# Down projection of 18 of 22 feature tiles as 2x2 blocks in 7 products, in one pipeline with the up projection

## The chip, the core and the metric

The kernel runs on one core of a Trainium2 chip. The metric is the device time of one execution, in microseconds (us). The kernel before takes 2363.89 us, the median of 3 runs that lie between 2362.02 and 2364.42 us.

## What is computed

Two layers on 1024 tokens of width 1024, in fp32. Each layer has a mixer (gated MLP and pooling in layer 0, two kinds of attention in layer 1) and a feed-forward part, with residual sums and norms between them. The change is in the feed-forward part alone:

```python
def conv_ffn(h, w_up, conv_w, conv_b, w_down):
    a, g = jnp.split(h @ w_up, 2, axis=-1)              # w_up: 1024 x 5632
    a = lax.conv_general_dilated(a, conv_w, ...) + conv_b   # causal, 3 taps per feature
    return (jax.nn.gelu(a) * g) @ w_down                # w_down: 2816 x 1024
...
h = h + conv_ffn(rms_norm(h, norm_ffn[layer]), ...)
```

The 2816 features are 22 tiles of 128.

## The kernel before

Activations lie with features on the partitions and tokens along the free axis. An fp32 product is made of three matmuls (`mm3`, L164 to L168): each operand x is split into hi, a rounded copy, and lo = x - hi, and hi·hi, hi·lo and lo·hi are summed in PSUM. The hi part is a ScalarE cast and the lo part a VectorE subtraction (`split`, L177 and L178, for activations; L355 and L359 for the weights of the up projection; L136 and L137 for other weights). A matmul has 128x128 weights and 512 tokens.

**Up** (`up`, L468). One step per feature tile j computes gate and value of that tile together, as a 2x2 block product in 7 instead of 8 products (`PRODUCTS`, L404). The blocks of the activations (b11, b21, d, e, t3, b22, t4) are sums of quarters of the normed input, made once per layer; the four combinations of weights ("forms" 0 to 3, `form`, L361) are made in each step for the next one. A product is 4 contraction tiles x 3 = 12 matmuls, a step 84. The order of products is 1, 2, 4, 3, 6, 5, 7, and `read` (L421) moves results out of PSUM between them. Behind product 7 comes `conv` (L450: two ScalarE passes, two VectorE passes), and in the next step, behind product 2, `gate` (L459), which multiplies by the gate and writes the 512 KB tile to `a_dram` in DRAM (L465). Steps 0 and 1 run interleaved while the blocks are made, parts of steps 2 and 3 (`early`) with them; from j = 2 on a loop runs the steps one after the other.

**Down.** The 22 tiles are taken in chunks of 2, 4, 4, 4, 4, 4. `fetch(c)` (L556) reads a chunk's tiles from `a_dram` and splits them, `down(c)` (L565) runs the plain product: 8 output tiles x 2 halves of the tokens x the chunk's tiles x 3 matmuls, and after each output tile's half a VectorE add of the PSUM bank into the residual tile x (L582). `residual` (L549) loads x, 16 transfers of 256 KB, in the last up step. In that step the first two fetches and the first weights are issued too. The last chunk also feeds the next norm.

All transfers named here are issued by SyncE (SP) in program order, and each waits there until its target buffer is free. A tile framework places each engine's instructions in an order that it works out from the program and its own cost estimates; ScalarE, VectorE, TensorE and SP each run theirs strictly in that order.

Layer 0's feed-forward lies at about 242 to 924 us of the trace, layer 1's at about 1660 to 2360 us. The last up step of layer 0 runs from 666.0 to 685.06 us, that of layer 1 from 2082.6 to 2101.7 us.

Of the kernel before, what the change touches and what calls it, by code (L numbers as in the profile page):

```python
# [10 lines left out]
F32 = mybir.dt.float32  # L11
F32R = mybir.dt.float32r
# [10 lines left out]
HF = 512  # L23
FF = 2816
NFF = FF // P
CHUNKS = (2, 4, 4, 4, 4, 4)
EPS = 1e-6
NEG = -1.0e30
LAMBDA_INIT = 0.8 - 0.6 * math.exp(-0.3)
# [31 lines left out]
def tile_block(  # L61
# [58 lines left out]
    a_dram = dram.tile([NFF, P, S], F32, name="a_dram")  # L120


    def w_tiles():
# [2 lines left out]
    class Weights:  # L126


        def __init__(self, src, ncol=2048):
            self.w = ncol // 2  # L130
            self.parts = []
            for i in range(2):
                raw = wraw_p.tile([P, self.w], F32, tag="raw", name="raw")
                nc.sync.dma_start(raw, src[:, i * self.w : (i + 1) * self.w])
# [132 lines left out]
    class FFN:  # L267
        def __init__(self, layer, stack):
            self.layer = layer
            hp = stack.enter_context(pool(name=f"ffh{layer}", bufs=1))  # L270
            self.raw_p = stack.enter_context(pool(name=f"ffr{layer}", bufs=4))
# [72 lines left out]
        def raw(self, j):  # L344
            f = self.forms[j] = {}
            for i, x in enumerate("ag"):
                f[x] = self.raw_p.tile([P, 1024], F32, tag="wr", name="wr")
                nc.sync.dma_start(f[x].rearrange("p (k c) -> p k c", c=P), self.columns(j, i))
# [12 lines left out]
        def form(self, j, n, part):  # L361

            if part == 1:
                return self.lo(j, n)
            if j not in self.forms or n == 1 and j in self.early:
                self.raw(j)
            f = self.forms[j]
            a, g = f["a"], f["g"]
            c0, c1 = slice(0, HF), slice(HF, S)
            if n == 0:  # L370
                self.hi(j, 0, a)
            elif n == 1:
                q = f["q"] = wraw_p.tile([P, 1024], F32, tag="raw", name="q")
# [35 lines left out]
        def product(self, j, n):  # L409
            st = self.st.setdefault(j, {})  # L410
            tile_n, block, b, opens = self.PRODUCTS[n]
            bank = {2: "y", 3: "z", 5: "z"}.get(n, "x")
            if opens:
                st[bank] = self.banks.pop(0)
            wh, wl, _ = self.forms[j][tile_n]
            bh, bl = self.B[b]
            for k in range(4):
                c = slice(block * HF + k * P, block * HF + (k + 1) * P)
                mm3(st[bank], wh[:, c], wl[:, c], bh[k // 2][:, k % 2, :], bl[k // 2][:, k % 2, :], opens and k == 0, k == 3, not opens)
            self.read(j, n, st)  # L420

        def read(self, j, n, st):

# [16 lines left out]
            elif n == 6:  # L440
                V.tensor_tensor(st[3], st["x"], st[3], op=ALU.add)

        def open_a(self, j):
            st = self.st[j]
            st["a"] = self.ep.tile([P, P + S], F32, tag="f_a", name="f_a", bufs=2)
            G.memset(st["a"][:, 0:2], 0.0)
            if j in self.early:
                A.copy(st["a"][:, 2 : 2 + HF], st[1])

        def conv(self, j):  # L450
            st, a = self.st[j], self.st[j]["a"]
            cw = PC_CW[self.layer] + 3 * j
            acc = st["acc"] = self.H[j % 4][0].rearrange("p a b -> p (a b)")
# [5 lines left out]
        def gate(self, j):  # L459
# [2 lines left out]
            V.scalar_tensor_tensor(acc[:, :HF], acc[:, :HF], -1.0, st["x"], op0=ALU.mult, op1=ALU.mult)  # L462
            self.banks.append(st["x"])
            V.scalar_tensor_tensor(acc[:, HF:], acc[:, HF:], -1.0, st[3], op0=ALU.mult, op1=ALU.mult)
            nc.sync.dma_start(a_dram[j], acc)  # L465

        def up(self):
            self.st = {}  # L468
# [31 lines left out]
            for j in both:  # L500
# [1 line left out]
                self.conv(j)  # L502
                self.gate(j)
                self.forms_of(2, 2 + j)
            for j in range(2, NFF):
                nxt = j + 1 if j + 1 < NFF else None

                def form(n, part):
                    if nxt is not None and not (n == 0 and nxt in self.early):
                        self.form(nxt, n, part)  # L510

                if j in self.early:
                    self.open_a(j)
                else:
                    self.product(j, 1)
                if j > 2:
                    self.form(j, 3, 1)
                if j not in self.early:
                    self.product(j, 2)
                if j > 2:  # L520
                    self.gate(j - 1)
                form(0, 0)
                if nxt is None:
                    self.fetch(0)
# [6 lines left out]
                self.product(j, 6)  # L531
                form(1, 1)
                if nxt is None:
                    self.residual(1)
                self.product(j, 5)
                form(2, 0)
                if nxt is None:
# [6 lines left out]
            self.gate(NFF - 1)  # L544


        FIRST = [sum(CHUNKS[:c]) for c in range(len(CHUNKS))]
# [8 lines left out]
        def fetch(self, c):  # L556

            if c >= len(CHUNKS):
                return
            for i in range(CHUNKS[c]):  # L560
                raw = self.raw_p.tile([P, 2, HF], F32, tag="wr", name="ar")
                nc.sync.dma_start(raw.rearrange("p a b -> p (a b)"), a_dram[self.FIRST[c] + i])
                split(hph[i][c % 2], hpl[i][c % 2], raw)

        def down(self, c, norm, after, follow):  # L565
            nj, tiles = CHUNKS[c], self.FIRST[c] // 2
            ncol = 2048 // nj
            last = c == len(CHUNKS) - 1
            ws = {}

            def mm(n, c0, w):
                wi = n * P // ncol
                if wi not in ws:
                    ws[wi] = get_w(w_dn[self.layer], tiles + wi, f"dn{self.layer}")
                ps = ps_acc("ps_d")[:, :w]
                half, o = c0 // HF, c0 % HF
                for i in range(nj):
                    x = n * P - wi * ncol
                    mm3(ps, *ws[wi](i * ncol + x, P), hph[i][c % 2][:, half, o : o + w], hpl[i][c % 2][:, half, o : o + w],
                        i == 0, i == nj - 1)  # L580
                h = self.xT[n][half][:, o : o + w]
                V.tensor_tensor(h, ps, h, op=ALU.add)  # L582
                if last:
                    norm.add(c0, n, h)

            if not last:
                for n in range(KT):
                    for half in range(2):
                        mm(n, half * HF, HF)
                return  # L590
# [8 lines left out]
        def run(self, after, follow=()):  # L599
# [1 line left out]
            with pool(name=f"ffe{self.layer}", bufs=1) as self.ep:  # L601
                self.up()
            with pool(name=f"ffm{self.layer}", bufs=1) as np_:
                norm = Norm(np_)
                for c in range(len(CHUNKS)):
                    if c > 0:
                        self.fetch(c + 1)
                    self.down(c, norm, after, follow)


    def out_proj(ff):
# [656 lines left out]
```

## Time and profile before

| | us |
|---|---|
| median of 3 runs | 2363.89 |
| the profiled execution | 2362.53 |
| its span, first to last instruction | 2360.8 |
| TensorE busy (matmuls) in it | 2301.3 |
| VectorE busy | 1550.0 |
| ScalarE busy | 957.1 |
| mean granted TensorE clock | 0.994 |

The profile is that of one execution. Its span is 1.7 us shorter than that execution's own time, which is 1.4 us under the median. Matmuls are pipelined: one of 512 columns is recorded with 0.39 us, but follows its neighbour by less, so starts are read, not durations. An engine's idle time counts only where the next engine on the chain waits for it. L followed by a number is a line of the kernel before; PE is TensorE, DVE VectorE, ACT ScalarE, SP SyncE, and ps_u and ps_d are the PSUM banks of the up and the down projection.

### The profile page before, as it was taken

What the parts mean: (1) busy time and instruction counts of PE and PEld (TensorE: products, weight loads), DVE (VectorE), ACT (ScalarE), POOL (GpSimd) and SP (SyncE); (2) the same over time, 40 slices, a digit from 0 to 9 for tenths busy, and PEclk for the clock granted to TensorE, in tenths of its full rate; (3) what the DMA queues carried; (4) which work ended last, traced back from release to release, by engine and by line L of the source; (5) the groups of instructions that cost most, each with busy time, mean ns of one, the idle gap of its engine ahead of it and who ended that gap; (6) DMA issues with size and microseconds to landing.
All of it is one profiled execution on the core that took longest, in us unless ns stands there. A gap on an engine that the chain in (4) does not pass through costs nothing.

```text
span 2360.8 us, 30644 instructions
## 1 busy us (share of the span) xinstructions
PE 2301.3 (97%) x11652; PEld 1943.7 (82%) x11652; DVE 1550.0 (66%) x2957; ACT 957.1 (41%) x1553; POOL 9.4 (0%) x67
## 2 busy tenths in 40 slices
PE   7999999999999999999999999999899999999997
PEld 7888878888888888897888888888678888888887
DVE  6673896666674447556445788896996666674446
ACT  6231353344341113546545556663453344341111
POOL 0000000000000000000000000000000000000000
PEclk9999999999999999999999999999899999999999
DMA  4115032222263213222212131234432222263211
GB/s 139 61 49 192 32 116 81 81 87 83 89 241 108 90 46 120 70 68 71 78 53 77 39 113 49 73 122 147 143 107 81 81 85 86 86 241 110 90 36 72
DMA packets 178226, 223.69 MB, mean 95 GB/s; under 512 B 11168, under 2 KB 126112, under 8 KB 178080
## 3 DMA queue, kind: packets, MB, share of 16 engines
q1 hardware_dynamic: 177216, 220.70, 28.5%
q8 instruction: 91, 1.49, 0.3%
q10 hardware_dynamic: 864, 1.04, 0.2%
q14 instruction: 55, 0.45, 0.1%
HBM read 162.88 MB, written 52.53 MB: 91 GB/s over the span
## 4 chain that ended last, share of the span: by engine, by line
PE 83%; DVE 8%; ACT 4%; DMA 3%; issue 2%; SPq 0%; DVEq 0%; ACTq 0%
PE ps_u L168 12%; PE ps_u L167 12%; PE ps_u L166 12%; PE ps_d L166 7%; PE ps_d L167 7%; PE ps_d L168 7%; PE ps_qk L168 3%; PE ps_qk L166 3%; PE ps_qk L167 3%; PE ps_o L166 2%; PE ps_o L168 2%; PE ps_o L167 2%; PE ps_vv L168 2%; PE ps_vv L167 2%; PE ps_vv L166 2%
## 5 line engine op out<-in xcount | busy, mean ns | idle before, releaser
L166 PE MATMUL ps_u<-hph,wh 128*128 128x512 f32 x768 | 300.2, 392 | 2.2 <-ACT hph L177 2.2
L167 PE MATMUL ps_u<-hpl,wh 128*128 128x512 f32 x768 | 299.9, 391 | 0.2 <-DVE hpl L178 0.2
L168 PE MATMUL ps_u<-hph,wl 128*128 128x512 f32 x768 | 299.9, 391 | 0.0
L166 PE MATMUL ps_d<-hph,wh 128*128 128x512 f32 (+1 forms) x736 | 279.8, 380 | 0.0
L167 PE MATMUL ps_d<-hpl,wh 128*128 128x512 f32 (+1 forms) x736 | 279.7, 380 | 0.0
L168 PE MATMUL ps_d<-hph,wl 128*128 128x512 f32 (+1 forms) x736 | 279.6, 380 | 0.0
L582 DVE TENSOR_TENSOR x<-ps_d,x 128x512 f32<-128x512 f32 (+1 forms) x200 | 131.8, 667 | 183.0 <-PE ps_d L168 182.8
L137 DVE TENSOR_TENSOR wl<-raw,wh 128x1024 fp32r<-128x1024 f32 (+1 forms) x110 | 132.1, 1201 | 168.8 <-ACT wh L136 168.5
L136 ACT CAST wh<-raw 128x1024 fp32r<-128x1024 f32 (+1 forms) x110 | 113.3, 1036 | 262.4 <-PE ps_d L167 176.8
L355 ACT CAST wh<-q 128x1024 fp32r<-128x1024 f32 x88 | 92.7, 1053 | 235.3 <-PE ps_u L167 211.7
L359 DVE TENSOR_TENSOR wl<-q,wh 128x1024 fp32r<-128x1024 f32 x88 | 107.7, 1224 | 117.8 <-ACT wh L355 117.8
L166 PEld LDWEIGHTS ps_u<-hph,wh 128*128 128x128 f32 x768 | 144.6, 189 | 32.7 <-ACT hph L177 2.6
L167 PEld LDWEIGHTS ps_u<-hpl,wh 128*128 128x128 f32 x768 | 144.9, 189 | 31.5 <-DVE hpl L178 1.3
L168 PEld LDWEIGHTS ps_u<-hph,wl 128*128 128x128 f32 x768 | 144.7, 188 | 30.4 <-DVE wl L359 0.4
L168 PEld LDWEIGHTS ps_d<-hph,wl 128*128 128x128 f32 x736 | 138.4, 188 | 26.4
L166 PEld LDWEIGHTS ps_d<-hph,wh 128*128 128x128 f32 x736 | 138.4, 188 | 26.4
L167 PEld LDWEIGHTS ps_d<-hpl,wh 128*128 128x128 f32 x736 | 138.4, 188 | 25.9
L166 PE MATMUL ps_qk<-hph,wh 128*128 128x512 f32 x384 | 151.9, 396 | 0.0
L168 PE MATMUL ps_qk<-hph,wl 128*128 128x512 f32 x384 | 151.7, 395 | 0.0
L167 PE MATMUL ps_qk<-hpl,wh 128*128 128x512 f32 x384 | 151.5, 395 | 0.0
L168 PE MATMUL ps_u<-x,wl 128*128 128x512 f32 x352 | 137.4, 390 | 1.1 <-DVE wl L359 1.1
L167 PE MATMUL ps_u<-x,wh 128*128 128x512 f32 x352 | 137.3, 390 | 1.1 <-DVE x L178 1.1
(253 smaller groups left out, 4943.3 us busy)
## 6 DMA issues: line engine op xcount, KB each, us to landing
wr<-in_w_up SPq DMA_DIRECT2D x88, 512.0 KB, 4.1
a_dram<-h SPq DMA_DIRECT2D x44, 512.0 KB, 2.6
ar<-a_dram SPq DMA_DIRECT2D x44, 512.0 KB, 4.9
raw<-in_w_dn SPq DMA_DIRECT2D x44, 512.0 KB, 4.3
raw<-in_w_oin SPq DMA_DIRECT2D x36, 512.0 KB, 3.6
h_dram<-h SPq DMA_DIRECT2D x32, 256.0 KB, 4.6
x<-h_dram SPq DMA_DIRECT2D x32, 256.0 KB, 5.6
raw<-in_w_ein SPq DMA_DIRECT2D x12, 512.0 KB, 4.4
```

What stands on the lines that cost most here:

```text
L136: A.copy(wh, raw)
L137: V.tensor_sub(wl, raw, wh.bitcast(F32))
L166: T.matmul(ps, lh, rh, start=first, stop=False, skip_group_check=more)
L167: T.matmul(ps, lh, rl, start=False, stop=False, skip_group_check=more)
L168: T.matmul(ps, ll, rh, start=False, stop=last, skip_group_check=more)
L355: A.copy(t[0], src)
L359: V.tensor_sub(l, src, h.bitcast(F32))
L582: V.tensor_tensor(h, ps, h, op=ALU.add)
```

## The change

The host's layout of `w_dn` becomes 11 pieces of two tiles. Eighteen of the 22 feature tiles, 9 pairs, go through the same 7-product scheme in the down projection, in 3 groups of 3 pairs. The steps of the loop in `up` run on from 22 to 33: each group has 4 steps, one for each pair of output tiles, and a step is 7 products of 3 pairs x 3 = 9 matmuls, 63 in all. Forms of the down weights are 768 columns wide instead of 1024 and are made by the same code. The remaining 4 tiles are done in the plain way at the end, with the norm.

The gated activations go to DRAM as split blocks: behind each odd step's gate, seven tasks (four for the last two pairs) are queued, and at most four of them run in one step, behind products 4, 3, 6 and 5. A task makes a sum of quarters (four of the seven have one), splits it into one of two stage tiles, and writes 512 KB to `g_dram`. The reads (`fetch`, 3 transfers of 512 KB per block, 21 per group) land in the 24 slots that held the blocks of the up projection. Those for a group are issued in the step ahead of it as its products free the slots.

```diff
-CHUNKS = (2, 4, 4, 4, 4, 4)
+CHUNKS = (2,) * 11
+GROUP = 3
+NGROUP = 3
...
         def raw(self, j):
...
+                group, m = divmod(j - NFF, 4)
+                f[x] = t[:, : 2 * GROUP * P]
+                src = w_dn[self.layer, group * GROUP : (group + 1) * GROUP].rearrange("i p (h c) -> h p i c", h=2)
+                for h in range(2):
+                    nc.sync.dma_start(f[x].rearrange("p (h i c) -> h p i c", h=2, c=P)[h],
+                                      src[h, :, :, (2 * m + i) * P : (2 * m + i + 1) * P])
...
+        def read_down(self, j, n, st):
+            m = (j - NFF) % 4
+            h = lambda r, half: self.xT[2 * m + r][half]
+            if n in (1, 3, 4, 6):
+                bank = st["z" if n == 3 else "x"]
+                t = self.ep.tile([P, HF], F32, tag="sb", name=f"f_s{n}", bufs=6)
+                A.copy(t, bank)
+            else:
+                t = st[{2: "y", 5: "z", 7: "x"}[n]]
+                self.banks.append(t)
+            to = {1: h(0, 0), 2: h(0, 0), 4: h(0, 1), 5: h(0, 1), 7: h(1, 0), 3: h(1, 1), 6: h(1, 1)}[n]
+            V.tensor_tensor(to, to, t, op=ALU.subtract if n in (3, 6, 7) else ALU.add)
...
         def gate(self, j):
...
-            nc.sync.dma_start(a_dram[j], acc)
+            if j % 2:
+                self.tasks += self.gated_blocks(j // 2, self.last, acc)
+            self.last = acc
...
+            def step(i, src, form):
+                if form is not None:
+                    form()
+                self.turn ^= 1
+                t = self.stage[self.turn]
+                split(t[:, 0, :].bitcast(F32R), t[:, 1, :].bitcast(F32R), src)
+                nc.sync.dma_start(g_dram[p, i], t)
...
+        def fetch(self, group, i):
+            for k in range(GROUP):
+                slot = (group * 7 + i) * GROUP + k
+                t = self.slot(slot)
+                self.gated.setdefault((group, self.BLOCKS[i]), []).append(t)
+                nc.sync.dma_start(t.bitcast(F32), g_dram[group * GROUP + k, i])
...
+            end = NFF + 4 * NGROUP
+            for j in range(2, end):
+                nxt = j + 1 if j + 1 < end else None
+                group = (j - NFF + 1) // 4 if (j - NFF) % 4 == 3 and j >= NFF - 1 else None
...
+                def used(i):
+                    if group is None:
+                        return
+                    if group == 0:
+                        for x in {0: (0,), 1: (1,), 3: (2, 3), 6: (4, 5, 6)}.get(i, ()):
+                            self.fetch(0, x)
+                    elif group < NGROUP:
+                        if i == 0:
+                            self.fetch(group, 0)
+                        if i < 6:
+                            self.fetch(group, i + 1)
+                    elif i < 2:
+                        self.rest(i + 1)
...
                 self.product(j, 4)
+                used(2)
+                self.task()
                 form(0, 1)
-                if nxt is None:
+                if j == NFF - 1:
                     self.residual(0)
                 self.product(j, 3)
+                used(3)
+                self.task()
...
-                if nxt is None:
-                    load_ahead(w_dn[self.layer], 0, f"dn{self.layer}")
-                    self.fetch(1)
                 self.product(j, 7)
-                self.conv(j)
+                used(6)
+                if j < NFF:
+                    self.conv(j)
```

The order of instructions moves at three places that matter here.

SP, from the last up step of layer 0 into the down projection, first as before (h_dram holds the residual, in_w_dn the down weights, ar is a raw gated tile):

```order
L465 DMA a_dram<-h_0_1659 128x1024
L554 DMA x_0_5043<-h_dram 128x512 x2
L554 DMA x_1_5044<-h_dram 128x512 x2
...
L554 DMA x_1_5085<-h_dram 128x512
L562 DMA ar<-a_dram 128x1024 x5
L465 DMA a_dram<-h_0_1661 128x1024
```

and the same place in the changed kernel (g_s and the h, hph and hpl tiles are slots for split blocks, wr raw weights of a step):

```order
L682 DMA x_1_5323<-h_dram 128x512
L543 DMA hph_1_87<-g_dram 128x1024
L543 DMA hpl_1_95<-g_dram 128x1024
...
L543 DMA h_1_2589<-g_dram 128x1024
L543 DMA g_s<-g_dram 128x1024
L364 DMA wr<-in_w_dn 128x3x128 x4
L529 DMA g_dram<-h_0_1665 128x1024
L529 DMA g_dram<-stage 128x1024
```

The weights of step 23 (the x4 row, two transfers for each of its two tiles) now stand behind all 21 fetches of group 0 and the 16 residual loads.

SP at the change from group 0 to group 1, in the changed kernel:

```order
L364 DMA wr<-in_w_dn 128x3x128 x4
L543 DMA h_0_5721<-g_dram 128x1024
L364 DMA wr<-in_w_dn 128x3x128 x6
L543 DMA hph_0_82<-g_dram 128x1024
L543 DMA hpl_0_90<-g_dram 128x1024
L543 DMA hph_0_84<-g_dram 128x1024
```

Eighteen fetches follow one another there, and the weights of the group's second step come behind them.

VectorE from up step 2 to 3, before (f_s and f_a take products out of PSUM, L438 that of product 5, and wl is the lo part of a form of weights):

```order
L464 SCALAR_TENSOR_TENSOR h_0_1661<-h_0_1661,f_s_2466 128x512
L374 TENSOR_TENSOR q<-wr 128x512
L441 TENSOR_TENSOR f_s_2683<-ps_u_2302,f_s_2683 128x512
L375 TENSOR_TENSOR q<-q,wr 128x512
L374 TENSOR_TENSOR q<-wr 128x512
L375 TENSOR_TENSOR q<-q,wr 128x512
L359 TENSOR_TENSOR wl<-q,wh 128x1024
L438 TENSOR_TENSOR f_a<-ps_u_2303,f_s_2386 128x512
```

and now (L185 is the lo part of a task's split, L514 its sum):

```order
L498 SCALAR_TENSOR_TENSOR h_0_1661<-h_0_1661,f_s_2466 128x512
L185 TENSOR_TENSOR stage<-h_0_1659,stage 128x512
L185 TENSOR_TENSOR h_0_1665<-h_0_1661,h_0_1665 128x512
L392 TENSOR_TENSOR q<-wr 128x512
L462 TENSOR_TENSOR f_s_2685<-ps_u_2302,f_s_2685 128x512
L393 TENSOR_TENSOR q<-q,wr 128x512
L514 TENSOR_TENSOR h_0_1659<-h_0_1659 128x512
L459 TENSOR_TENSOR f_a<-ps_u_2303,f_s_2386 128x512
L376 TENSOR_TENSOR wl<-q,wh 128x1024
```

Two splits, a sum and product 5's eviction stand ahead of the lo part that step 3 multiplies with.

## Rows read from the trace of the kernel before

**Rows 1.** The page's head and its first part: busy time, share of the span, instructions.

```profile
span 2360.8 us, 30644 instructions
PE 2301.3 (97%) x11652; PEld 1943.7 (82%) x11652; DVE 1550.0 (66%) x2957; ACT 957.1 (41%) x1553; POOL 9.4 (0%) x67
```

**Rows 2.** Timeline of PE, layer 0: two matmuls 24 apart, at product boundaries.

```profile
451.14 0.39 PE L166 MATMUL ps_u<-hph,wh 128*128 128x512 f32 x1
...
456.58 0.39 PE L166 MATMUL ps_u<-hph,wh 128*128 128x512 f32 x1
```

**Rows 3.** Groups of the down projection: busy us, mean ns | idle before them, releaser.

```profile
L168 PE MATMUL ps_d<-hph,wl 128*128 128x512 f32 x672 | 261.4, 389 | 0.0
...
L582 DVE TENSOR_TENSOR x<-ps_d,x 128x512 f32<-128x512 f32 x184 | 125.3, 689 | 182.1 <-PE ps_d L168 182.1
```

**Rows 4.** Timeline of PE, last matmul of up and first of down, layer 0.

```profile
684.83 0.39 PE L168 MATMUL ps_u<-h,wl 128*128 128x512 f32 x1
685.06 0.39 PE L166 MATMUL ps_d<-hph,wh 128*128 128x512 f32 x1
```

**Rows 5.** Groups, shapes apart: casts, splits and copies of 512 and 1024 columns.

```profile
L359 DVE TENSOR_TENSOR wl<-q,wh 128x1024 fp32r<-128x1024 f32 x88 | 107.7, 1224 | 117.8 <-ACT wh L355 117.8
...
L355 ACT CAST wh<-q 128x1024 fp32r<-128x1024 f32 x88 | 92.7, 1053 | 235.3 <-PE ps_u L167 211.7 <-DVE q L375 11.3 <-DVE q L380 7.8
...
L427 ACT COPY f_s<-ps_u 128x512 f32<-128x512 f32 x88 | 50.5, 575 | 11.9 <-PE ps_u L168 9.0 <-DVE n_y L188 2.9
...
L359 DVE TENSOR_TENSOR wl<-wr,wh 128x512 fp32r<-128x512 f32 x44 | 30.0, 684 | 0.0
...
L355 ACT CAST wh<-wr 128x512 fp32r<-128x512 f32 x44 | 27.3, 623 | 21.3 <-PE ps_u L167 21.3
```

**Rows 6.** Stretches (us, busy by engine, PEclk, DMA share, GB/s): an up step; steps 2, 3.

```profile
456.58:475.62 19.04, 19.04 (x86) 15.77 (x84) 12.53 (x16) 7.54 (x10) 0.10 (x1) 1.00 0.27 83
1738.00:1757.00 19.00, 19.00 (x86) 15.70 (x85) 17.36 (x24) 8.70 (x12) 0.10 (x1) 1.00 0.47 155
```

**Rows 7.** DMA issues: KB each, median us from issue to landing.

```profile
a_dram<-h SPq DMA_DIRECT2D x44, 512.0 KB, 2.6
```

**Rows 8.** Timeline of SP's queue around the end of up, layer 0.

```profile
673.01 10.05 SPq L554 DMA_DIRECT2D x<-h_dram  x16
```

**Rows 9.** Stretches of dense transfers around the end of up, both layers (columns as Rows 6).

```profile
679.00:692.00 13.00, 13.00 (x59) 10.78 (x58) 9.32 (x12) 4.77 (x5) 0.00 (x0) 1.00 1.00 384
687.00:692.00 5.00, 5.00 (x24) 4.14 (x23) 3.96 (x6) 2.11 (x2) 0.00 (x0) 1.00 1.04 421
...
694.00:705.00 11.00, 11.00 (x50) 9.10 (x49) 9.43 (x13) 4.21 (x4) 0.00 (x0) 1.00 0.91 317
...
2104.00:2109.00 5.00, 5.00 (x24) 4.14 (x23) 4.00 (x6) 2.11 (x2) 0.00 (x0) 1.00 1.01 414
```

**Rows 10.** Timeline of DVE, up steps 2 to 3, layer 1.

```profile
1742.60 0.69 DVE L374 TENSOR_TENSOR q<-wr 128x512 f32<-128x512 f32 x1 [1.09 <-DMA wr<-in_w_up]
...
1743.93 1.22 DVE L359 TENSOR_TENSOR wl<-q,wh 128x1024 fp32r<-128x1024 f32 x1
1745.07 0.68 DVE L438 TENSOR_TENSOR f_a<-ps_u,f_s 128x512 f32<-128x512 f32 x1
```

**Rows 11.** Timeline of PE there: the first matmul of step 3 that needs that lo part.

```profile
1745.84 0.39 PE L168 MATMUL ps_u<-x,wl 128*128 128x512 f32 x1
```

**Rows 12.** Stretches at the start of layer 1's up projection: TensorE's granted clock.

```profile
1662.00:1668.00 6.00, 0.00 (x0) 0.00 (x0) 5.64 (x19) 3.53 (x5) 0.00 (x0) 0.60 1.12 343
...
1677.00:1680.00 3.00, 3.00 (x9) 2.32 (x8) 3.00 (x5) 1.90 (x2) 0.00 (x0) 0.50 0.00 0
...
1683.00:1690.00 7.00, 7.00 (x32) 5.79 (x32) 5.04 (x14) 2.77 (x4) 0.00 (x0) 1.00 0.01 3
```

More of the change, by code (lines that the diff above doesn't have):

```diff
@@ L129, in __init__ @@
         def __init__(self, src, ncol=2048):
+            if not isinstance(src, list):
+                src = [src[:, i * ncol // 2 : (i + 1) * ncol // 2] for i in range(2)]
             self.w = ncol // 2
             self.parts = []
-            for i in range(2):
+            for x in src:
                 raw = wraw_p.tile([P, self.w], F32, tag="raw", name="raw")
-                nc.sync.dma_start(raw, src[:, i * self.w : (i + 1) * self.w])
+                nc.sync.dma_start(raw if len(x.shape) == 2 else raw.rearrange("p (k c) -> p k c", k=x.shape[1]), x)
                 wh, wl = (t[:, : self.w] for t in w_tiles())
@@ L372, in form @@
             elif n == 1:
[L373 removed]
+                q = f["q"] = wraw_p.tile([P, 1024], F32, tag="raw", name="q")[:, :w]
                 V.tensor_add(q[:, c0], g[:, c0], g[:, c1])
@@ L415, in product @@
             wh, wl, _ = self.forms[j][tile_n]
[L416 to L420, printed above, removed]
+            if j < NFF:
+                b = [[t[k // 2][:, k % 2, :] for t in self.B[b]] for k in range(4)]
+            else:
+                b = [[t[:, x, :] for x in range(2)] for t in self.gated[(j - NFF) // 4, b]]
+            for k, (bh, bl) in enumerate(b):
+                c = slice((block * len(b) + k) * P, (block * len(b) + k + 1) * P)
+                mm3(st[bank], wh[:, c], wl[:, c], bh, bl, opens and k == 0, k == len(b) - 1, not opens)
+            (self.read if j < NFF else self.read_down)(j, n, st)
         def read(self, j, n, st):
@@ L464, in gate, with gated_blocks @@
             V.scalar_tensor_tensor(acc[:, HF:], acc[:, HF:], -1.0, st[3], op0=ALU.mult, op1=ALU.mult)
-            nc.sync.dma_start(a_dram[j], acc)
+            if j % 2:
+                self.tasks += self.gated_blocks(j // 2, self.last, acc)
+            self.last = acc
+        ORDER = (1, 2, 4, 3, 6, 5, 7)
+        BLOCKS = ("b11", "b21", "e", "d", "t3", "b22", "t4")
+        def gated_blocks(self, p, a, b):
+            half = [slice(0, HF), slice(HF, S)]
+            a0, a1, b0, b1 = (t[:, c] for t in (a, b) for c in half)
+            if p < GROUP * NGROUP:
+                steps = [
+                    (0, a0, None), (1, b0, None),
+                    (3, a0, lambda: V.tensor_sub(a0, a0, a1)),
+                    (2, a0, lambda: V.scalar_tensor_tensor(a0, a0, -1.0, b1, op0=ALU.mult, op1=ALU.subtract)),
+                    (5, b1, None),
+                    (4, a1, lambda: V.tensor_sub(a1, b1, a1)),
+                    (6, b0, lambda: V.scalar_tensor_tensor(b0, a0, -1.0, b0, op0=ALU.mult, op1=ALU.subtract)),
+                ]
+            else:
+                steps = [(i, t, None) for i, t in enumerate((a0, b0, a1, b1))]
+            def step(i, src, form):
[5 more added lines that the diff above has]
+                nc.sync.dma_start(g_dram[p, i], t)
+            return [functools.partial(step, *x) for x in steps]
@@ new lines, in task, with slot @@
+        def task(self):
+            if self.tasks:
+                self.tasks.pop(0)()
+        def fetch(self, group, i):
[4 more added lines that the diff above has]
+                nc.sync.dma_start(t.bitcast(F32), g_dram[group * GROUP + k, i])
+        def slot(self, n):
+            n %= 24
+            if n not in self.slots:
+                if n < 16:
+                    q, x = divmod(n, 4)
+                    t = (hph, hpl)[x % 2][(q % 2) * 2 + x // 2][q // 2]
+                elif n == 16 + 4:
+                    t = self.ep.tile([P, 2, HF], F32R, tag="f_a", name="g_s", bufs=2)
+                elif n < 20:
+                    t = self.B["t4"][(n - 16) % 2][(n - 16) // 2]
+                else:
+                    t = self.tile("h", n - 21, 0, F32R)
+                self.slots[n] = t
+            return self.slots[n]
@@ L467, in up, with rest @@
+        def rest(self, i):
+            for n, x in ((15, 0), (16, 1), (17, 2)) if i == 0 else ((18, 3), (19, 4)) if i == 1 else ((21, 5), (22, 6), (23, 7)):
+                half, t = divmod(x, 4)
+                p, r = divmod(t, 2)
+                self.plain[t, half] = self.slot(n)
+                nc.sync.dma_start(self.plain[t, half].bitcast(F32), g_dram[GROUP * NGROUP + p, 2 * half + r])
         def up(self):
-            self.st = {}
+            self.st, self.tasks, self.gated, self.slots, self.plain, self.turn = {}, [], {}, {}, {}, 0
+            self.stage = [self.H[3][0], None]
@@ L504, in up @@
                 self.forms_of(2, 2 + j)
-            for j in range(2, NFF):
-                nxt = j + 1 if j + 1 < NFF else None
+            self.stage[1] = self.raw_p.tile([P, 2, HF], F32, tag="st", name="stage", bufs=1)
+            end = NFF + 4 * NGROUP
+            for j in range(2, end):
+                nxt = j + 1 if j + 1 < end else None
+                group = (j - NFF + 1) // 4 if (j - NFF) % 4 == 3 and j >= NFF - 1 else None
                 def form(n, part):
@@ L510, in form @@
                         self.form(nxt, n, part)
+                def used(i):
[11 more added lines that the diff above has]
+                        self.rest(i + 1)
+                if group == NGROUP:
+                    self.rest(0)
                 if j in self.early:
@@ L515, in up @@
                     self.product(j, 1)
+                used(0)
                 if j > 2:
@@ L554, in residual, with down @@
                     nc.sync.dma_start(self.xT[kt][half], h_dram[kt, :, half * HF : (half + 1) * HF])
[L556 to L569, printed above, removed]
+        def down(self, norm, after, follow):
+            first = GROUP * NGROUP
+            src = [w_dn[self.layer, p].rearrange("p (h c) -> p h c", h=2) for p in (first, first + 1)]
+            ws = [load_w([x[:, :, i * HF : (i + 1) * HF] for x in src]) for i in range(2)]
             def mm(n, c0, w):
-                wi = n * P // ncol
-                if wi not in ws:
-                    ws[wi] = get_w(w_dn[self.layer], tiles + wi, f"dn{self.layer}")
                 ps = ps_acc("ps_d")[:, :w]
                 half, o = c0 // HF, c0 % HF
[L577 to L580, printed above, removed]
+                for i in range(4):
+                    t = self.plain[i, half]
+                    mm3(ps, *ws[n // 4](i * HF + n % 4 * P, P), t[:, 0, o : o + w], t[:, 1, o : o + w], i == 0, i == 3)
                 h = self.xT[n][half][:, o : o + w]
                 V.tensor_tensor(h, ps, h, op=ALU.add)
[L583 to L590, printed above, removed]
+                norm.add(c0, n, h)
             for c0, w in ((0, HF), (HF, HF)) if follow else ((0, HF), (HF, HF // 2), (HF + HF // 2, HF // 2)):
@@ L603, in run @@
             with pool(name=f"ffm{self.layer}", bufs=1) as np_:
[L604 to L608, printed above, removed]
+                self.down(Norm(np_), after, follow)
     def out_proj(ff):
```

31 lines of the change are left out of this document (19 added, 12 removed).

## The prediction

> **What bounds the kernel now.** The page's first part comes first: matmuls fill 97% of the span, VectorE 66%, ScalarE 41% [rows 1]. So the time is the number of matmuls times their distance, plus the gaps between them. The timeline of TensorE gives the distance: two matmuls 24 apart start 5.44 us apart, 0.2267 us each [rows 2]. An up step of 84 is therefore 19.04 us. Next, the groups of the down projection: no idle time stands before its matmuls, and VectorE's evictions there wait for TensorE 182.1 us in all, not the other way round [rows 3]. Even between up and down nothing is lost, the matmuls on both sides are 0.23 us apart [rows 4]. So fewer matmuls save their full time, as long as everything else keeps up; the question is what now has to keep up.
>
> **What it removes.** In 8 products a 2x2 block product takes as many matmuls as the plain one. Per layer 9 pairs of feature tiles x 4 pairs of output tiles x 8 products x 3 = 864 matmuls of 512 columns become 756. 108 x 0.2267 = 24.5 us per layer, **-49.0 us** in both. Nothing hides this, since down has no idle time before its matmuls [rows 3]. A down step is 63 x 0.2267 = 14.28 us, a product in it 2.04 us.
>
> **The steady steps.** An up step has 12.5 us of VectorE work and 7.5 of ScalarE in 19.04 [rows 6]. The tasks add at most four splits per step, 3.5 in the mean, and two sums: at 0.69 us on VectorE and 0.62 on ScalarE a split [rows 5] that makes some 16 and 9.7 us. Both fit. Order could still hurt: the copy of product 4 must leave the bank before product 6 adds to it, and only product 3 (2.72 us) lies between; a task's cast (0.62), a weight cast (1.05) and the copy itself (0.58) [rows 5] make 2.25, which leaves 0.5. A down step has four copies (2.3 us) and casts of three and a half forms on ScalarE, and on VectorE seven adds (4.8 us), four form sums and the lo parts, some 10 us in 14.28. Between nothing and 10 us, I take **+3**, nearest to the first, as the spare time in the rows is larger than the load that is added. Queues: the writes go from 0.5 MB per up step to about 1.8 MB, beside 1 MB of weights, with the DMA engines 27% busy before [rows 6].
>
> **Start of up (steps 2 and 3).** Here VectorE is nearly full already, 17.4 of 19 us [rows 6]. The lo part that step 3's product 4 needs ends at 1743.93 + 1.22 = 1745.15 [rows 10], and is used at 1745.84 [rows 11]: 0.69 us spare. Four splits and two sums add 3.7 us to that stretch; the sums for step 4, which waited 1.09 us for a transfer there [rows 10], now come later. 17.4 + 3.7 - 1.2 = 19.9 in 19, so 0.9 us are missing, and product 5's eviction now stands ahead. Between 0 and 4 per layer, I take 1.5: **+3**.
>
> **The turn from up to down.** This is the term that decides. In the last up step SP issues 21 fetches of 512 KB and 16 residual loads of 256 KB, which count as 29 transfers of 512 KB, and only behind them the weights of step 23 (step 22's were loaded ahead). Before, the same place had the residual and single raw tiles. Let d be the time of 512 KB in a full queue. The stream can begin when the first slots come free: 6 matmuls (1.36 us), and about 1.2 us until bytes move; a lone write takes 2.6 us to land [rows 7], of which 512 KB at the full rate are under 1.3. So 2.6 us into step 21. Then 29 d, then 384 KB of weights (0.75 d), 0.4 us for the landing to be seen (estimate, a third of that lead), and 0.85 us for a cast of 768 columns, between the 0.62 and 1.05 of 512 and 1024 [rows 5]. Step 23 should start 19.04 + 14.28 = 33.3 us after step 21. The stall is T0 = 2.6 + 29.75 d + 1.25 - 33.3 = 29.75 d - 29.45. The tasks' writes stand behind these transfers and their split waits there too, but off the matmuls.
>
> What is d? The residual alone was issued at 16 in 10.05 us [rows 8], 1.26 us per 512 KB. Stretches of dense transfers run at 414 to 421 GB/s over 5 us, 384 over 13 us and 317 over 11 us [rows 9], which is d = 1.25, 1.37 and 1.66. The first are reads without writes, the last mixes reads, a write and small gaps, with the engines 91% busy. The new stream is pure reading for 40 us with 13 us as the nearest row, so I take **d = 1.37**: T0 = 11.3 us, both layers **+22.6**. The ends are 7.7 and 19.9 per layer.
>
> A rule speaks against this d. The Trainium skill, DMA: Bandwidth & Descriptors, section "Where 436 GB/s comes from", says that between HBM and SBUF the HBM side binds at about 358 GB/s; an estimate from its figure is d = 1.46, and a sum of 2359 us in place of 2350. The 384 and 421 GB/s of [rows 9] disagree with it as a ceiling.
>
> **The two changes of group.** 18 fetches in a row, starting 0.68 us (3 matmuls) + 1.2 us into the group's last step, then the next weights as above, and the step that needs them starts 28.56 us after: T1 = 1.88 + 18.75 d + 1.25 - 28.56 = 18.75 d - 25.43. At 1.37 this is 0.3, so a shorter chain decides: the lo part of the next step's form 0 stands on VectorE behind the eviction of product 7, 0.69 + 0.95 (768 columns, between 0.69 and 1.22, [rows 5]), less the two matmuls that don't need it (0.45): 1.2 us. Four such places, **+4.8**. The ends are 1.2 each and, at d = 1.66, 5.7.
>
> **The clock.** After the idle stretch before up in layer 1 (no matmul from 1662 to 1668) TensorE's granted clock is 0.50, the lower level of 1.2 GHz: 9 matmuls in 3 us where the full one would do 13, until some 1680 [rows 12]. T0's gaps are split over several products, with matmuls between. Between 0 and 3 us per layer, I take 1: **+2**.
>
> **At no cost:** the plain rest (its weights and 8 blocks are issued a step ahead and down had no idle time), the norm, the residual loads, the host's layout.
>
> **The sum** against the profiled execution: -49.0 + 3 + 3 + 22.6 + 4.8 + 2 = -13.6, 2362.5 to 2348.9. That execution was 1.4 us under the median, so **2350 us**. At d = 1.25 (T0 7.7) it is 2343; at d = 1.66 2385. A change under 0.2%, 4.7 us, can't be told from none here.
>
> **Rivals.**
> 1. *The stream runs like the slow stretch.* If reading back what was just written, with writes and weights in between, holds 317 GB/s, T0 is 19.9 and T1 5.7: -49 + 39.8 + 22.8 + 8 = +21.6, **2385 us, slower**. For it: the 11 us after the residual are the only row where gated tiles are read back [rows 9]. Against: the gaps there come from SP waiting for buffers, and the engines are busy 91%. It decides from where -49 + 2 (29.75 d - 29.45) + 4 (18.75 d - 25.43) + 8 is zero: d = 1.50, 350 GB/s. Chance 0.13.
> 2. *The stream is a little slower than the 13 us row*, d around 1.46: T0 14.1, T1 2.0, so -49 + 28.2 + 8 + 8 = -4.8, **2359 us, hardly told from no change**. For it: the rate falls from 421 to 384 as the stretch gets longer [rows 9], and 40 us are longer still. Chance 0.17. This is also where the page's 358 GB/s would put it.
> 3. *The task's split gets ahead of the copy of product 4 and the lo parts in the up steps.* The spare 0.5 us above goes, and each step with tasks loses 0.6 us, a split's time: 2 x 18 steps, +21.6 on the forecast, **2372 us, slower**. For it: each engine runs strictly in its order, and gelu (over 1 us) also stands there. Against: VectorE is idle a third of such a step [rows 6]. It decides when ScalarE is 0.5 us late. Chance 0.12.
> 4. *The turn costs little*, if the stream starts much earlier than I think or step 22's own weights and blocks are all that is waited for. Then T0 is about nothing, **2328 us**. Against: at 421 GB/s 29 transfers take 36 us, and there are 33. Chance 0.08.
> 5. *The change does not do what it says*: the matmuls in the built program are 216 fewer, 2 x 108, so no chance is kept for it.
>
> **How the numbers follow.** The forecast has 0.50, the rivals 0.13, 0.17, 0.12 and 0.08. The forecast's own cases, d from 1.25 to 1.45, give 2343 to 2357. Faster is the forecast and rival 4 and a few hundredths of rival 2: 0.60. Same is most of rival 2 and a little of the forecast's upper end, 0.16. Slower is rivals 1 and 3 with what of 2 lies over the line, 0.24. The range from 2335 to 2380 leaves out rival 4 and most of rival 1, 0.2 in all.
>
> **What would show it.** In the new profile: TensorE's busy time about 49 us lower; no idle time before the matmuls of up steps 4 to 20; gaps of some 11 us in all between the last up step and the second down step of each layer, in products that wait for fetched blocks and then for the weights of step 23, with the DMA engines over 95% busy at about 380 to 390 GB/s; four gaps of 1 to 2 us at the changes of group, where matmuls wait for wl; VectorE at 18 to 19 of 19 us in steps 2 and 3. Wrong would be: gaps in steps with tasks that wait for VectorE or ScalarE (rival 3), a rate under 350 GB/s (rival 1), or a turn without a gap (rival 4).

## The result, and the profile after

The changed kernel takes 2342.64 us, the median of 4 runs (2341.33 to 2343.87), beside 2363.06 us before on the same chip: 0.9914, with a 95% interval of 0.9902 to 0.9927. That is 20.4 us faster, where 13.6 were forecast; 2342.6 lies in the range given (2335 to 2380), near the forecast's own lower case of 2343.

The page's head and first part, which answer to [rows 1]:

```profile
span 2339.5 us, 31344 instructions
PE 2262.5 (97%) x11436; PEld 1903.1 (81%) x11436; DVE 1709.4 (73%) x3291; ACT 1080.5 (46%) x1807; POOL 9.4 (0%) x67
```

There are 216 matmuls fewer, VectorE has 159 us more to do and ScalarE 123 us more. TensorE's recorded busy time falls by 38.8 us only, not by the 49 that were to show it: some 20 matmuls at the lower clock, seen below, are recorded longer (some 4 us), and a recorded matmul of 0.39 us covers the first 0.16 us of each new gap. So the gaps are better taken from starts: I sum, over a stretch, what lies between one matmul's start and the next beyond the 0.227 us of [rows 2], where it is over 0.02 us.

| stretch, gaps in us | before | after |
|---|---|---|
| up, steps 2 and 3 as the loop runs them, layers 0 and 1 | 1.0, 1.3 | 0.9, 1.4 |
| up, steps 4 to 20 | 0.0, 0.0 | 0.1, 1.3 |
| last up step to the start of the second down step | 0.0, 0.0 | 10.9, 11.0 |
| changes of group (two per layer) | 0.0, 0.0 | 2.1, 3.0 |
| rest of the second down step, third down step | 0.0, 0.0 | 0.2, 0.2 |

Unrounded, the new gaps come to 28.7 us. -49.0 + 28.7 is -20.3, and the span is 21.3 us shorter; the rest lies outside these stretches.

The waits of TensorE on ps_u (us in total, times, the longest) name whom it waited for:

```profile
PE ps_u L173 <- DMA hph<-g_dram: 9.7, 2, 4.9
PE ps_u L173 <- ACT wh L372: 5.4, 6, 1.1
...
PE ps_u L173 <- DMA h<-g_dram: 1.7, 6, 0.4
```

Two long waits are for fetched tiles, one per layer. Six, of about 1 us, are for a cast of weights (L372): two at the turns and four at the changes of group. TensorE's timeline at the turn in layer 0 shows both kinds (start, length, and the idle time before it with its releaser):

```profile
698.31 0.76 PE L173 MATMUL ps_u<-hph,wh 128*128 128x512 f32 x1 [4.77 <-DMA hph<-g_dram]
...
706.92 0.50 PE L173 MATMUL ps_u<-h,wh 128*128 128x512 f32 x1 [0.23 <-DMA h<-g_dram]
...
708.20 0.50 PE L173 MATMUL ps_u<-g_s,wh 128*128 128x512 f32 x1 [0.30 <-DMA g_s<-g_dram]
...
710.22 0.50 PE L173 MATMUL ps_u<-hph,wh 128*128 128x512 f32 x1 [1.06 <-ACT wh L372]
```

Product 6 of step 22 waits for the first of the three tiles of its block, product 7 takes each of its tiles as it lands, and step 23 waits for its weights. That cast had itself waited for the transfer, as ScalarE's timeline says, at the turn and at a change of group:

```profile
709.34 0.83 ACT L372 CAST wh<-wr 128x768 fp32r<-128x768 f32 x1 [6.22 <-DMA wr<-in_w_dn]
...
767.82 0.83 ACT L372 CAST wh<-wr 128x768 fp32r<-128x768 f32 x1 [3.29 <-DMA wr<-in_w_dn]
```

Stretches of the kernel after, columns as in [rows 6]: the stream at the first turn, the wait there and the matmuls behind it, the stream at the second turn and the slow matmuls there, a change of group and the matmuls behind it, a steady up step and steps 2 to 3 of both layers:

```profile
668.70:708.00 39.30, 33.85 (x134) 26.24 (x132) 18.20 (x26) 11.46 (x16) 0.00 (x0) 0.91 1.02 399
675.00:708.00 33.00, 27.55 (x106) 21.01 (x104) 13.17 (x18) 7.98 (x12) 0.00 (x0) 0.90 1.04 411
...
693.40:698.30 4.90, 0.14 (x1) 0.02 (x1) 0.69 (x1) 0.59 (x1) 0.00 (x0) 0.90 1.05 419
698.30:704.00 5.70, 5.69 (x14) 4.25 (x15) 0.69 (x1) 0.59 (x1) 0.00 (x0) 0.50 1.02 419
...
2074.20:2114.00 39.80, 33.47 (x135) 25.47 (x134) 18.59 (x26) 11.45 (x16) 0.00 (x0) 0.96 1.03 397
2104.00:2107.00 3.00, 3.00 (x8) 2.24 (x9) 0.00 (x0) 0.00 (x0) 0.00 (x0) 0.50 1.02 419
740.00:767.00 27.00, 27.00 (x121) 22.37 (x120) 14.90 (x23) 7.63 (x12) 0.00 (x0) 1.00 0.97 372
767.00:772.00 5.00, 4.23 (x19) 3.01 (x18) 3.01 (x5) 1.99 (x3) 0.00 (x0) 1.00 1.08 379
...
456.58:475.62 19.04, 19.04 (x85) 15.77 (x85) 17.16 (x23) 10.46 (x14) 0.10 (x1) 1.00 0.41 139
1725.00:1744.00 19.00, 19.00 (x84) 15.74 (x85) 19.00 (x28) 10.71 (x16) 0.10 (x1) 1.00 0.68 238
320.00:339.00 19.00, 18.47 (x82) 14.96 (x82) 19.00 (x27) 11.24 (x17) 0.12 (x2) 1.00 0.68 231
```

Through both turns the DMA engines are in the mean fully busy (share 1.02 and 1.03), at 397 to 399 GB/s. An up step has 17.2 us of VectorE work where it had 12.5, still under its 19.04; at the start of up VectorE is busy without a break.

### The profile page after: what moved, and what is told of

It reads as the page before. It is cut to its first block, busy times and chain, and to the rows that moved or that the text cites. A ratio compares the mean times of both kernels' runs of the same rounds, so it can differ in the third digit from the quotient of the medians.

```text
span 2339.5 us, 31344 instructions
## 1 busy us (share of the span) xinstructions
PE 2262.5 (97%) x11436; PEld 1903.1 (81%) x11436; DVE 1709.4 (73%) x3291; ACT 1080.5 (46%) x1807; POOL 9.4 (0%) x67
## 4 chain that ended last, share of the span: by engine, by line
PE 72%; DVE 10%; DMA 10%; ACT 5%; issue 2%; SPq 0%; DVEq 0%; ACTq 0%
PE ps_u L173 14%; PE ps_u L175 13%; PE ps_u L174 13%; PE ps_qk L175 3%; PE ps_qk L173 3%; PE ps_qk L174 3%; DMA wr<-in_w_dn 2%; DMA hph<-g_dram 2%; PE ps_o L173 2%; PE ps_o L175 2%; PE ps_o L174 2%; PE ps_vv L175 2%; PE ps_vv L173 2%; PE ps_vv L174 2%; PE av_c L1013 1%
## 5 line engine op out<-in xcount | busy, mean ns | idle before, releaser
L173 PE MATMUL ps_u<-hph,wh 128*128 128x512 f32 x960 | 376.8, 393 | 14.5 <-DMA hph<-g_dram 9.7
L175 PE MATMUL ps_u<-hph,wl 128*128 128x512 f32 x960 | 375.2, 392 | 0.0
L174 PE MATMUL ps_u<-hpl,wh 128*128 128x512 f32 x952 | 372.1, 391 | 0.2 <-DVE hpl L185 0.2
L372 ACT CAST wh<-q 128x1024 fp32r<-128x1024 f32 (+1 forms) x136 | 132.8, 977 | 180.1 <-PE ps_u L174 119.6
L376 DVE TENSOR_TENSOR wl<-q,wh 128x1024 fp32r<-128x1024 f32 (+1 forms) x136 | 153.6, 1130 | 44.6 <-ACT wh L372 43.9
L174 PE MATMUL ps_u<-x,wh 128*128 128x512 f32 x352 | 137.3, 390 | 1.0 <-DVE x L185 1.0
L173 PE MATMUL ps_u<-x,wh 128*128 128x512 f32 x352 | 136.8, 390 | 0.0
L372 ACT CAST wh<-wr 128x1024 fp32r<-128x1024 f32 (+3 forms) x132 | 100.7, 769 | 68.5 <-PE ps_u L174 37.7
L173 PE MATMUL ps_u<-h,wh 128*128 128x512 f32 x288 | 113.5, 394 | 5.5 <-ACT wh L372 3.3
L376 DVE TENSOR_TENSOR wl<-wr,wh 128x1024 fp32r<-128x1024 f32 (+3 forms) x132 | 114.6, 873 | 1.2 <-ACT wh L372 1.1
L174 PE MATMUL ps_u<-h,wh 128*128 128x512 f32 x288 | 112.3, 391 | 1.1 <-DVE h L185 1.1
L175 PE MATMUL ps_u<-h,wl 128*128 128x512 f32 x288 | 112.3, 390 | 0.0
```

Source lines behind the costliest of these rows:

```text
L173: T.matmul(ps, lh, rh, start=first, stop=False, skip_group_check=more)
L174: T.matmul(ps, lh, rl, start=False, stop=False, skip_group_check=more)
L175: T.matmul(ps, ll, rh, start=False, stop=last, skip_group_check=more)
L372: A.copy(t[0], src)
L376: V.tensor_sub(l, src, h.bitcast(F32))
```

## The experiments

The theory to test, after the trace: the kernel gained 108 matmuls per layer in full and gave back what one transfer queue takes too long for, at the turn and at the changes of group; what the change put on VectorE, ScalarE and the clock costs next to nothing. Rivals are named with each run. Ratios are to the kernel before, measured beside each run on the same chip; it took 2360.6 to 2363.1 us there, so the times of runs that have different ones beside them compare to some 2 us.

**1. Twelve of the sixteen residual loads later.** `residual` loads two output tiles at a time; the first pair stays in the last up step, the others go to the first two down steps.

```diff
-            for kt in range(4 * i, 4 * i + 4):
+            for kt in range(2 * i, 2 * i + 2):
...
                 if j == NFF - 1:
                     self.residual(0)
+                if j == NFF:
+                    self.residual(1)
                 self.product(j, 3)
...
-                if j == NFF - 1:
-                    self.residual(1)
+                if j in (NFF, NFF + 1):
+                    self.residual(2 + j - NFF)
```

> Of the 16 residual loads only the first 4 stay in the last up step; the other 12 are issued in the first two down steps, behind the weights of the second. Theory A (the turn is paced by the queue: 21 fetches, 16 residual loads and the weights one after another): 12 x 256 KB fewer ahead of the weights of step 23, 6 x 1.27 to 1.31 us = 7.6 to 7.9 us per layer, so the 10.8 us of stall at each turn fall to about 3 and the time from 2342.6 to about 2327 us. Rival B (the turn is paced by slots that come free only with product 7 of the last up step, and by the blocks of step 22 itself): less than half of that, 2336 us or more.

Measured: 2325.95 us, 0.9848 (0.9833 to 0.9863). At the turns the gaps are 3.2 and 2.7 us instead of 10.9 and 11.0, 16.0 less for 24 loads of 256 KB, 1.33 us per 512 KB (in a second run, below, 3.9 and 3.8 us, so 1.2). The long wait is gone; what is left are the last tiles and the weights, in the trace of this run:

```profile
697.60 0.47 PE L173 MATMUL ps_u<-h,wh 128*128 128x512 f32 x1 [0.37 <-DMA h<-g_dram]
...
702.05 0.50 PE L173 MATMUL ps_u<-hph,wh 128*128 128x512 f32 x1 [1.08 <-ACT wh L372]
```

So the turn is paced by the order and length of the queue, not by slots.

Some of the gain comes back: 0.2 us per layer vanish behind the start of the second down step, and 1.0 us are new in the third. In layer 0 its weights are late by 0.4 us of that; the rest is the chain of the prediction, a lo part (L376) that stands on VectorE behind the eviction of product 7, as in layer 1:

```profile
2113.12 0.69 DVE L475 TENSOR_TENSOR x<-x,ps_u 128x512 f32<-128x512 f32 x1 [1.35 <-PE ps_u L175]
2113.73 0.95 DVE L376 TENSOR_TENSOR wl<-wr,wh 128x768 fp32r<-128x768 f32 x1
```

The cast for this lo part was done at 2112.34, while VectorE was idle.

**2. One block behind the weights at the changes of group.**

```diff
-                        if i < 6:
+                        if i < 5:
                             self.fetch(group, i + 1)
...
                 form(0, 0)
+                if j in (NFF + 4, NFF + 8):
+                    self.fetch((j - NFF) // 4, 6)
                 self.product(j, 4)
```

> At the two changes of group the last block's three fetches are issued behind the weights of the step that waits there, instead of ahead of them. Theory A (the four stalls there, 5.1 us in all by the trace, are weights that come late behind 18 fetches): three fetches fewer ahead, 3.8 us, so all four stalls go to nearly nothing and the time to about 2338 us. Rival B (my prediction's chain: eviction of product 7, then the lo part on VectorE, 1.2 us whatever the queue does): the stalls stay, 2342 us.

Measured: 2339.13 us, 0.9900 (0.9884 to 0.9917), an interval that overlaps that of the changed kernel (0.9902 to 0.9927). The time would suit theory A; the trace does not. The waits for a cast fall from six to the two at the turns, but beside the two waits for a lo part at the start of up, which the changed kernel has too, stand four new ones at the changes of group:

```profile
PE ps_u L175 <- DVE wl L376: 4.0, 6, 0.7
...
PE ps_u L173 <- ACT wh L372: 2.1, 2, 1.1
```

and VectorE's timeline shows why:

```profile
764.24 0.69 DVE L475 TENSOR_TENSOR x<-x,f_s 128x512 f32<-128x512 f32 x1 [1.35 <-ACT f_s L470]
765.60 0.69 DVE L475 TENSOR_TENSOR x<-x,ps_u 128x512 f32<-128x512 f32 x1 [0.68 <-PE ps_u L175]
766.21 0.95 DVE L376 TENSOR_TENSOR wl<-wr,wh 128x768 fp32r<-128x768 f32 x1
```

The cast that the lo part needs ran on ScalarE at

```profile
764.10 0.84 ACT L372 CAST wh<-wr 128x768 fp32r<-128x768 f32 x1
```

and was done at 764.94; VectorE was idle until 765.60, but its next instruction was the eviction of product 5, and the lo part behind it came at 766.21. The gaps at the four changes are 4.1 us in all, against 5.1. So rival B, the chain that I had forecast at 1.2 each, is there, at 1.0 and with another eviction; in the changed kernel the late weights merely ended a little after it.

**3. Two blocks behind the weights, with experiment 1.** Experiment 1's edit, and experiment 2's with the last two blocks in the later place:

```diff
-                        if i < 6:
+                        if i < 4:
                             self.fetch(group, i + 1)
...
                 form(0, 0)
+                if j in (NFF + 4, NFF + 8):
+                    self.fetch((j - NFF) // 4, 5)
+                    self.fetch((j - NFF) // 4, 6)
                 self.product(j, 4)
```

This puts the lo part ahead of that eviction. Beside it, the edits of experiments 1 and 2 together, and experiment 1 again.

> The late residual loads and the last block behind the weights, together. Theory A (the turn and the changes of group are separate stretches of the queue, so their gains add): 2326 less the 3.5 us that the second gave alone, about 2322.5 us. Rival B (the loads that were moved into the first group's steps push its successor's fetches, so the changes of group get worse and the gains don't add): 2326 us or more.

> Late residual loads as in the first experiment, and at the changes of group the last two blocks (six fetches) behind the weights. In the build the lo part of form 0 now stands ahead of product 5's eviction on VectorE. Theory A' (after one block was moved, the 1.0 us left at each change was that eviction plus the lo part, no longer the queue): the four gaps there go, 4.0 us less than with one block and 5 to 6 less than the late residual alone, about 2321 us. Rival B (moving fetches only moves the wait: products 5 and 7 of the new group then wait for their blocks): gaps of 1 us or more in the new group's first step, 2326 us or more.

> The first experiment's kernel once more, on the same chip as the one above, so that the two can be compared: 2326 us.

Measured: one block and the late residual 2327.59 us, 0.9854 (0.9839 to 0.9869), no gain over experiment 1 in the time; its gaps at the changes of group are 4.1 us, those of experiment 1 6.4, a difference that is below the intervals. Two blocks: 2322.62 us, 0.9840 (0.9827 to 0.9854), and experiment 1 on the same chip 2328.48 us, 0.9864 (0.9850 to 0.9877). The gaps at the four changes are 1.0 us in all. VectorE's order at the first of them is now

```profile
755.19 0.69 DVE L475 TENSOR_TENSOR x<-x,f_s 128x512 f32<-128x512 f32 x1 [1.40 <-ACT f_s L470]
755.92 0.96 DVE L376 TENSOR_TENSOR wl<-wr,wh 128x768 fp32r<-128x768 f32 x1
```

with 0.1 us lost before the first matmul that reads wl. New gaps of 1 us in the group's first step are not there, so the wait did not move on. This kernel is the fastest of the study, 1.6% under the kernel before; that it beats experiment 1 by 5.9 us is borne out by the trace with some 5 us (experiment 1's two runs have 6.4 and 5.7 us at the changes of group), while the two intervals overlap slightly.

**4. The clock at the turn.** Matmuls that nobody reads fill the gap ahead of product 6.

```diff
                 form(1, 0)
+                if j == NFF:
+                    spare, (wh, wl, _) = self.banks[-1], self.forms[j][0]
+                    for i in range(21):
+                        T.matmul(spare, wh[:, :P], self.gated[0, "b11"][0][:, 0, :], start=i == 0, stop=i == 20)
                 self.product(j, 6)
```

> 21 matmuls whose result nobody reads (4.8 us) are put ahead of product 6 of the first down step, into the gap of 4.9 us in which TensorE waits for the third-last block. They should keep TensorE from falling to its lower clock there. Theory A (the queue paces the turn, so the 2 us that slow matmuls take there are hidden): no change, 2342 to 2343 us, with the slow matmuls gone from the trace. Rival B (the lower clock costs what it adds to the matmuls): 12 x 0.2 us in layer 0 and 9 x 0.2 us in layer 1 come back, about 2338.5 us.

Measured: 2342.35 us, 0.9918 (0.9904 to 0.9933). The same two stretches as above, in this run:

```profile
693.40:698.30 4.90, 4.70 (x21) 3.57 (x19) 0.69 (x1) 0.59 (x1) 0.00 (x0) 1.00 1.05 418
698.30:704.00 5.70, 4.24 (x14) 2.35 (x15) 0.69 (x1) 0.59 (x1) 0.00 (x0) 1.00 1.02 419
```

The granted clock stays at 1.00, the upper level of 2.4 GHz, where it had been 0.50; 14 matmuls take 4.24 us instead of 5.69, and the time is the same. Product 6 now waits for each slot instead. The slow matmuls at the turn cost nothing, as the queue delivers a slot in 1.2 us with the clock at either level.

**5. The products put back.** An eighth product of 9 matmuls in each down step, its result unread.

```diff
                 form(1, 0)
+                if j >= NFF:
+                    spare, (wh, wl, _) = self.banks[-1], self.forms[j][0]
+                    for i in range(9):
+                        T.matmul(spare, wh[:, :P], self.gated[(j - NFF) // 4, "b11"][0][:, 0, :], start=i == 0, stop=i == 8)
                 self.product(j, 6)
```

> Each down step gets an eighth product of 9 matmuls whose result nobody reads, ahead of product 6: 2 x 12 x 9 x 0.2267 = 49.0 us of matmuls, which undoes the saving alone. Theory A (the stalls at the turns and group changes are set by the queue, so longer steps eat into them): step 22's extra product lies in the gap at the turn (2.0 us per layer back), and a group's last two steps give the queue 4.1 us more, which ends the 5.1 us of stalls there: +49.0 - 4.1 - 5.1 = +40, about 2382.5 us. Rival B (the gaps are independent of TensorE's pace): +49, 2391.6 us.

Measured: 2382.55 us, 1.0088 (1.0073 to 1.0103), 39.9 us more than the changed kernel. The total is theory A's, the shares are only partly so: the gaps at the turns fall by 1.9 and 2.5 us, as they should, but those at the changes of group from 5.1 to 4.1 only, since the lo part's chain of experiment 2 takes over there. The rest of what the trace has less (7.6 us over the whole span) lies in small gaps elsewhere, 1.3 of it in layer 1's up steps. So without the saved matmuls the new pipeline would be 0.9% slower than the kernel before.

**6. More work on VectorE and on ScalarE.** Each task's subtraction, or its cast, is done twice.

```diff
                 split(t[:, 0, :].bitcast(F32R), t[:, 1, :].bitcast(F32R), src)
+                V.tensor_sub(t[:, 1, :].bitcast(F32R), src, t[:, 0, :])
```

> Every task does its VectorE subtraction twice (the second gives the same values), 142 more in all. Theory A (VectorE has 17.2 of 19.04 us of work in a steady up step and is full in steps 2 and 3, so 3.5 x 0.6 us more just exceed a step): 0.3 us in some 36 steps and 2 us at each start, 2353 to 2358 us. Rival B (the 1.9 us to spare take it in): 2343 us. Rival C (every subtraction added stands ahead of something that TensorE waits for): 142 x 0.6 us, over 2400 us.

> Every task does its ScalarE cast twice, 142 more in all. Theory A (ScalarE has 10.4 of 19.04 us of work in a steady up step, and the copy of product 4 is not what ends last): no change, 2342 to 2344 us. Rival B (the third rival of my prediction: 0.5 us to spare between product 4's copy and product 6, which a second cast of 0.62 us uses up): 0.1 to 0.6 us in some 36 steps, 2347 to 2365 us.

The second kernel has `A.copy(t[:, 0, :].bitcast(F32R), src)` ahead of the split instead. Measured: subtraction twice 2347.61 us, 0.9938 (0.9922 to 0.9955), 5 us more, though the interval just overlaps that of the changed kernel; cast twice 2344.23 us, 0.9925 (0.9910 to 0.9940), no difference that can be told. The steady step with the subtraction twice:

```profile
456.58:475.62 19.04, 19.04 (x86) 15.77 (x85) 18.97 (x27) 10.01 (x14) 0.10 (x1) 1.00 0.45 155
```

VectorE is at 18.97 of 19.04 us, and yet steps 4 to 20 have no gap at all, in either layer. What it costs shows elsewhere: 1.5 us per layer in steps 2 and 3, 0.7 and 0.8 us at the turns, and 0.6 per layer later in the second down step. So theory A had the starts about right (2 us each), and the 36 steady steps take it in, as rival B said; no theory had the turns. The cast twice (12.5 of 19.04 us on ScalarE) adds nothing in the steady steps that can be told: 1.2 us of gaps in steps 4 to 20 of both layers, where the changed kernel has 1.3. So the third rival of the prediction falls at its price, 0.6 us in each step with tasks.

## Why the prediction came out right, and where it was off

- **The saving**, -49.0. The matmuls are 216 fewer, and putting them back cost 39.9 us where a sum that lets the gaps shrink gave 40. Right.
- **The turn**, 22.6 forecast, 21.9 by the trace. The mechanism is shown: moving 6 of the 29 d per layer out of the queue's way took 16 us off the two turns. The size came out by two errors with opposite signs, so its closeness is in part luck. The rate was higher than I took it: 411 GB/s over 33 us, 399 with the stream's first 6 us, d = 1.28 to 1.31 where I took 1.37 from the 13 us row. By the formula that gives 8.6 to 9.5 per layer, and 10.9 came. The landings of the fetches in the trace show where the rest lies. The first fetch lands 3.5 us after its issue and the third 6.6, where the formula with d = 1.28 has 2.9 and 5.4; and in layer 0 one later fetch lands 2.4 us after the one before it, where most land 1.2 to 1.3 apart. Why, the traces do not show.

  The Trainium skill, DMA: Bandwidth & Descriptors, section "Where 436 GB/s comes from", says that between HBM and SBUF the HBM side binds at about 358 GB/s. The trace disagrees: 399 GB/s stood for 39 us.
- **The changes of group**, 4.8 forecast, 5.1 by the trace. The size was right and the releaser wrong, so this too is luck: I let VectorE's chain decide, and the weights came later than that. With d = 1.31 my formula has them in time. In the trace the 18th fetch lands 26.3 to 27.1 us after the first one's issue, where the formula has 25.2; again the first lands late (3.4 to 3.5 us), and two or three of the others land 1.7 to 2.7 us after the one before, where most take 1.2 to 1.3. Experiment 2 then showed VectorE's chain just behind, and experiment 3 ended it.
- **The start of up**, +3 forecast, nothing by the trace: the failed step is "17.4 + 3.7 - 1.2 = 19.9 in 19, so 0.9 us are missing" (with the rows' own 0.69 for each of six instructions and 1.09 for the wait it would be 20.4). VectorE is indeed busy 19.0 of 19.0 us, but the wait of TensorE there is the same 0.70 us as before. A full engine delayed only work that nobody waited for.
- **The steady steps**, +3 forecast, 1.4 by the trace, all but 0.1 of it in layer 1; the traces of experiments 1 to 3, which have the same steps, have between nothing and 1.0. The forecast's sign, no idle time in steps 4 to 20, thus came nearly true. VectorE's load, put at 16 us, is 17.2, and experiment 6 shows the room: it takes 18.97 us of work in a step without a gap. The largest gap, 0.9 us in step 11 of layer 1, has the third rival's chain on ScalarE, with the copy of product 3 before product 5 in place of that of 4 before 6. A task's cast waits for the write that still reads its stage tile, the weight cast and the copy (L448) follow in order, and product 5 starts when the copy ends:

```profile
1891.94 0.62 ACT L184 CAST h<-h 128x512 fp32r<-128x512 f32 x1 [3.03 <-DMA g_dram<-h]
1892.47 1.05 ACT L372 CAST wh<-q 128x1024 fp32r<-128x1024 f32 x1
1893.42 0.58 ACT L448 COPY f_s<-ps_u 128x512 f32<-128x512 f32 x1
...
1894.05 0.50 PE L173 MATMUL ps_u<-hph,wh 128*128 128x512 f32 x1 [0.59 <-ACT f_s L448]
```

- **The clock**, +2 forecast, nothing. It did fall to 0.50 at both turns, and that cost nothing, since those matmuls wait for slots of the queue (experiment 4). The step that failed was to price it as if TensorE set the pace there.

The forecast was 7 us too high because three terms of 8 us together, each a risk that a row had shown, were paid in a place with cover, and cost some 1.4. The rivals: 1 and 2 fell with the rate, 4 with the gaps at the turn. The chain of 3 does occur, but at 1.3 us in all and not at 21.6.

## What to carry to other kernels

When matmuls are saved by fetching more, price the transfers of the transition as one queue: count what stands ahead of the first thing that is needed, multiply by the time per transfer of the longest dense stretch in the trace, and see what could be issued later; here 12 loads per layer that were needed only one to three steps later cost 16 us in both layers. The start of such a stream is a term of its own; here it took about 1 us more than the lead of a lone transfer had suggested. An engine that becomes full, or a clock that falls, costs something only where the next wait on the chain is for it, so add such a term only behind a named wait. And a stall with two causes close together moves its owner when one is removed: the wait's releaser before and after tells that, the time alone did not.

## What the hardware showed

The one queue held 399 GB/s over 39.3 us of reading into SBUF with the DMA engines fully busy, and delivered a slot of 512 KB in 1.2 us at the turn, which is more than the 384 GB/s of the 13 us row [rows 9]. In the six streams of 18 or more fetches the first tile landed 3.4 to 3.5 us after its issue and the second 1.4 to 2.7 us behind it, while most of the rest landed 1.2 to 1.3 us apart. TensorE's granted clock was 0.50 for its first matmuls after the gap of 4.9 to 5.1 us at each turn, while the gaps of about 1 us at the changes of group left it at 1.00.
